# LayerNorm 1 of a transformer trunk: rows normalised by ScalarE, gamma and beta applied behind the transpose and again by GpSimd on the way down

## The chip, the cores and the metric

The kernel runs on one core of a Trainium2 chip. The metric is the time of the whole kernel on the device in microseconds (us), as the median of several executions; lower is better. The engines are PE (TensorE, matmuls and transposes), DVE (VectorE), ACT (ScalarE), POOL (GpSimd) and SP (SyncE, which here issues all the transfers). Each engine works through its own list of instructions strictly in order.

## The reference

One layer on x of 1024 rows by 1024 columns, all in float32. Two attentions share one input projection; their projected outputs are gated and added, and one output projection follows. Then come two residual LayerNorms with a SwiGLU feed-forward (FFN) of 2816 hidden columns between them:

```python
mix = (gate_a * y_a + gate_b * y_b) @ w_out[l]
x = layer_norm(DEEPNORM_ALPHA * x + mix, ln1_g[l], ln1_b[l])
gu = x @ w_ffn_in[l]
g, u = jnp.split(gu, 2, axis=-1)
ffn = (jax.nn.silu(g) * u) @ w_ffn_out[l]
x = layer_norm(DEEPNORM_ALPHA * x + ffn, ln2_g[l], ln2_b[l])
```

Here layer_norm subtracts a row's mean, divides by its standard deviation, multiplies by gamma and adds beta, both of which belong to columns. The LN1 output is used twice: as the FFN's input and, scaled by DEEPNORM_ALPHA, as the residual of LN2.

## The kernel before, in words

Rows are handled in eight tiles of 128 (0 to 7), columns in two halves of 512, LO and HI. All large products are made with a Strassen-like scheme of seven half-size products, run in the order 5, 1, 3, 6, 2, 7, 4. Each float32 operand is split into a high part (a cast by ACT, L112) and a low part (the difference, by DVE, L113), and each product is three matmuls. A list scheduler fixes the order of every engine's instructions when the kernel is built, from its own costs; names such as op, yt, kp or QKV are sets of SBUF buffers, and a tile waits until its buffer is free.

The stages: input projection and gates, attention, output projection (`ops`, L1134, to about 788 us), LN1 and its transposes, FFN up (L179, 22 blocks of hidden columns, to 1219 us), FFN down (`dn`, L1275), LN2.

**LN1.** When a row tile's last product is taken from PSUM (L1125, L1127), DVE makes the statistics (L968, L969), adds epsilon (L970), and POOL raises the variance to the power -0.5 (L971). DVE then does (t - mean) * gamma on the full row (L972). In tiles 1 to 3 and 5 to 7 DVE goes on with times 1/std plus beta in two halves (L975); in tiles 0 and 4 ACT scales (L979) and POOL adds beta (L980). The finished row is stored to DRAM for the residual (`x1_dr`). When four row tiles are done, PE transposes them in 128x128 blocks (L995, `x1ps`), two banks of 512 for each of four steps. From each bank ACT casts the high part and DVE subtracts for the low part (`x1A`, `split`, L112 and L113). ACT also copies the first half's banks to `x1raw` (L1002) and four of the second half's to `x1s` (L1012), 16 casts and 12 copies in all; DVE makes sums of these (L1013, L1014, L1020, L1021), which are split again into the other products' operands.

**FFN up to down.** DVE and ACT make the hidden activations h; POOL makes sums of them (`sa`, `sb`, L1072 to L1078), which go to DRAM (`left_dr`).

**FFN down.** 77 steps, eleven for each product, each of 12 matmuls (L1275). A step needs a left operand `dl` (from `raw`, reloaded h sums) and a right operand `dr` (from `rows`, the weights, or from sums of these: `t` on L1237, `rows` on L1239 and L1240). Each is cast by ACT and subtracted by DVE, into a ring of eight buffers (QKV), so operands of four steps are held at a time. SP loads the rows nine steps ahead. Steps 3 to 10 of the first product each also load one row tile of the LN1 output (L1313, tiles 4 to 7, then 0 to 3) as `x`. After each product DVE takes its four banks from PSUM: the first product into the HI half of tiles 4 to 7, the second into the LO half of tiles 0 to 3 (L1125, alpha * x + bank).

Of the kernel before, what the change touches and what calls it, by code (L numbers as in the profile page):

```python
# [48 lines left out]

@with_exitstack  # L50
def hybrid_trunk_kernel(ctx: ExitStack, tc, x, xt, w_in, w_v, b_gate, rel_bias, w_proj,
                        w_out, ln1_g, ln1_b, w_ffn_in, w_ffn_out, ln2_g, ln2_b, out):

# [57 lines left out]
    def split(dst_h, dst_l, src):  # L111
        nc.scalar.copy(dst_h, src)  # L112
        nc.vector.tensor_tensor(dst_l, src, dst_h.bitcast(F32), ALU.subtract)  # L113
# [185 lines left out]
    def small_inputs():  # L299

        rel_sb = cycle(QK, "rel_sb")[0:8, 0:896]
        rel_in = cycle(QK, "rel_in")[0:8, 0:N_REL]
# [4 lines left out]
        dma(bg, b_gate)

    def store_hl(d, hi, lo):
        for h in range(2):  # L310
# [650 lines left out]
        dma(t, bass.AP(tensor=src.tensor, offset=src.offset, ap=[[0, P], [1, D]]))  # L961
        return t

    def layer_norm(t, g, b, name, quick, done=lambda cs: None):
        st = sml.tile([P, 12], F32, name=f"bn_{name}", tag="bn")
        mv = sml.tile([P, 3], F32, name=f"mv_{name}", tag="mv")
        for hf in range(2):
            nc.vector.bn_stats(st[:, 6 * hf:6 * hf + 6], t[:, hf * HW:(hf + 1) * HW])  # L968
        nc.vector.bn_aggr(mv[:, 0:2], st)  # L969
        nc.vector.tensor_scalar(mv[:, 2:3], mv[:, 1:2], EPS, None, ALU.add)  # L970
        nc.gpsimd.tensor_tensor(mv[:, 2:3], mv[:, 2:3], neghalf, ALU.pow)  # L971
        nc.vector.scalar_tensor_tensor(t, t, mv[:, 0:1], g, ALU.subtract, ALU.mult)  # L972
        if quick:
            for cs in (LO, HI):
                nc.vector.scalar_tensor_tensor(t[:, cs], t[:, cs], mv[:, 2:3], b[:, cs],  # L975
                                               ALU.mult, ALU.add)
                done(cs)
        else:
            nc.scalar.activation(t, t, AF.Copy, scale=mv[:, 2:3])  # L979
# [8 lines left out]
    def x1_operands(hf, acc_t):

        for kt in range(4):  # L990
            tps = []
            for k in (kt, kt + 4):
                tp = bank("tr", f"x1ps{hf}_{k}")
                for j in range(4):
                    tr(tp[:, j * P:(j + 1) * P], acc_t[4 * hf + j][:, k * P:(k + 1) * P], ident)  # L995
                tps.append(tp)
            if hf == 0:
                raw = slot("bw", f"x1raw{kt}")
                for i in range(2):
# [4 lines left out]
                x1raw.append(raw)
            else:
                raw = x1raw[kt]
                for i in range(2):
# [1 line left out]
                    split(o[:, LO], o[:, HI], tps[i])
                    ops_hi[i].append((o[:, LO], o[:, HI]))  # L1010
                s13 = slot("kp", f"x1s13_{kt}")
                nc.scalar.copy(s13[:, LO], tps[1])  # L1012
                nc.vector.tensor_tensor(s13[:, HI], raw[:, LO], tps[0], ALU.subtract)  # L1013
                nc.vector.tensor_tensor(s13[:, LO], tps[0], s13[:, LO], ALU.add)  # L1014
                x1s13.append(s13)
# [366 lines left out]
```

## Time and profile before

| what | value |
|---|---|
| median of three runs | 1431.96 us |
| lowest and highest run | 1430.93 and 1436.22 us |
| the profiled execution | 1438.71 us |
| its span in the trace | 1436.9 us |
| PE, DVE, ACT, POOL busy | 1405.3, 1024.1, 689.4, 309.9 us |
| granted TensorE clock, mean | 0.996 of full speed |

A row of a timeline has the start in us, the duration, the engine, the line, the operation, the tiles written and read, their shapes, and in brackets the idle time before it with what ended that. Back-to-back instructions of an engine overlap a little, so the distance of two starts is shorter than a duration. Rows of one kind are put together with their count (x3), and a count can be a little low, since some matmul records are missing. A grouped row has the total busy time, the mean of one in ns, and the idle time before the group with what ended most of it. Idle time of an engine that nobody waits for costs nothing.

### The profile page before, as it was taken

The numbers are of one execution on the slowest core, as the hardware profiler recorded it, in microseconds if no ns is written. First come the engines' busy times: TensorE is split into PE (matmuls) and PEld (weight loads), VectorE is DVE, ScalarE is ACT, GpSimd is POOL, SyncE is SP. The second block draws the span as 40 slices with busy tenths as digits, with TensorE's granted clock in tenths as the row PEclk, the third lists the DMA queues.
The fourth block names the chain that finished last, engine by engine and source line by source line (L and its number), as shares of the span: only waits on it lengthen the run. The fifth ranks groups of instructions, "written<-read, shape, count | busy, mean of one in ns | idle before, by whom it ended". The sixth has DMA issues, their size and how long they took to land.

```text
span 1436.9 us, 18884 instructions
## 1 busy us (share of the span) xinstructions
PE 1405.3 (98%) x6592; PEld 1159.7 (81%) x6592; DVE 1024.1 (71%) x1596; ACT 689.4 (48%) x1203; POOL 309.9 (22%) x365
## 2 busy tenths in 40 slices
PE   8999999999999998999999999999999999999997
PEld 6888888888778787888888878888888888888886
DVE  8866467773887987897779995555555544785996
ACT  6444354554888876783233543333333332444540
POOL 0000000000565775771303031111111100300012
PEclk9999999999999999999999999999999999999999
DMA  7565737888787559888862143223322227853521
GB/s 249 169 179 181 234 91 275 300 320 302 201 234 226 168 161 278 269 269 301 312 236 85 69 139 125 94 104 110 110 87 91 95 100 251 316 192 110 174 81 73
DMA packets 102895, 264.49 MB, mean 184 GB/s; under 512 B 10880, under 2 KB 27264, under 8 KB 102800
## 3 DMA queue, kind: packets, MB, share of 16 engines
q1 hardware_dynamic: 102800, 263.29, 55.3%
q8 instruction: 52, 0.85, 0.2%
q14 instruction: 43, 0.35, 0.1%
HBM read 172.25 MB, written 90.99 MB: 183 GB/s over the span
## 4 chain that ended last, share of the span: by engine, by line
PE 83%; DVE 8%; DMA 3%; ACT 3%; issue 2%; POOL 1%; POOLq 0%; SPq 0%; DVEq 0%; ACTq 0%
PE dn L1275 15%; PE sxf L179 14%; PE sxp L179 8%; PE szf L179 6%; PE v L431 5%; PE ops L1134 5%; PE szp L179 4%; PE gps L572 4%; PE syf L179 4%; PE yAps L793 2%; PE syp L179 2%; PE tp_b L730 2%; PE tp_a L730 1%; DMA wRf<-in_w_ffn_in_dram 1%; DMA yh<-y_dr2h 1%
## 5 line engine op out<-in xcount | busy, mean ns | idle before, releaser
L1275 PE MATMUL dn<-dr,dl 128*128 128x512 f32 x924 | 209.6, 389 | 0.0
L1275 PEld LDWEIGHTS dn<-dr,dl 128*128 128x128 f32 x924 | 173.4, 188 | 36.0
L704 POOL TENSOR_TENSOR w_b<-w_b,kp_b 128x511 f32<-128x511 f32 (+3 forms) x96 | 103.8, 1085 | 53.0 <-DVE kp_b L701 49.5
L701 DVE TENSOR_TENSOR_SCAN kp_b<-kp_b,ident_ps 128x512 f32<-128x512 f32 (+3 forms) x96 | 92.7, 966 | 4.0 <-ACT kp_b L699 1.4
L112 ACT CAST dl<-raw 128x512 fp32r<-128x512 f32 x77 | 47.5, 623 | 84.7 <-PE dn L1275 68.6
L1134 PE MATMUL ops<-wr,wl 128*128 128x512 f32 x336 | 78.8, 392 | 0.0
L971 POOL TENSOR_TENSOR mv<-mv,neghalf 128x1 f32<-128x1 f32 x16 | 25.6, 1603 | 242.0 <-DVE mv L970 242.0
L1134 PEld LDWEIGHTS ops<-wr,wl 128*128 128x128 f32 x336 | 62.5, 188 | 12.5
L653 POOL MEMSET bias<- 64x64 f32 x8 | 1.2, 146 | 330.1 <-ACT bias L652 330.1
L113 DVE TENSOR_TENSOR dl<-raw,dl 128x512 fp32r<-128x512 f32 x77 | 53.3, 699 | 24.8 <-ACT dl L112 24.2
L674 POOL TENSOR_SCALAR w_a<-w_a,st_a 128x640 f32<-128x640 f32 (+2 forms) x64 | 46.6, 734 | 75.9 <-PE sc_a L634 38.5
L113 DVE TENSOR_TENSOR pt_b<-tp_b,pt_b 128x512 fp32r<-128x512 f32 (+1 forms) x80 | 49.9, 630 | 16.7 <-ACT pt_b L112 15.8
L112 ACT CAST pt_b<-tp_b 128x512 fp32r<-128x512 f32 (+1 forms) x80 | 44.2, 554 | 36.6 <-PE tp_b L730 36.2
L1072 POOL TENSOR_TENSOR sb<-h 128x512 f32<-128x512 f32 x10 | 20.2, 2021 | 185.6 <-PE syf L179 135.1
L179 PE MATMUL szf<-x1S63h,wcf 128*128 128x512 f32 x168 | 55.1, 389 | 0.0
L192 DVE TENSOR_TENSOR gt<-sxf,gt 128x512 f32<-128x512 f32 x21 | 14.4, 686 | 54.9 <-PE sxf L179 54.9
L671 ACT ACTIVATE w_a<-w_a,st_a 128x640 f32<-128x640 f32 (+2 forms) x64 | 44.7, 699 | 13.2 <-DVE st_a L666 11.8
L699 ACT ACTIVATE kp_b<-sc_b 128x512 f32<-128x512 f32 (+3 forms) x96 | 49.0, 511 | 1.5 <-PE sc_b L634 1.4
L700 ACT ACTIVATE w_b<-sc_b 128x511 f32<-128x511 f32 (+3 forms) x96 | 49.1, 512 | 0.0
L1073 POOL TENSOR_TENSOR sa<-h,h 128x512 f32<-128x512 f32 x10 | 15.9, 1586 | 143.0 <-PE sxf L179 120.3
L730 PEld LDWEIGHTS tp_b<-ident,w_b 128*128 128x128 f32 x288 | 36.6, 141 | 12.1 <-issue 1.0
L730 PE MATMUL tp_a<-ident,w_a 128*128 128x128 f32 x240 | 41.9, 277 | 4.4 <-POOL w_a L674 2.5
(1525 smaller groups left out, 4188.2 us busy)
## 6 DMA issues: line engine op xcount, KB each, us to landing
raw<-left_dr SPq DMA_DIRECT2D x77, 256.0 KB, 2.9
wo_dr<-wo SPq DMA_DIRECT2D x28, 512.0 KB, 3.9
wr<-wo_dr SPq DMA_DIRECT2D x28, 512.0 KB, 8.7
wLf<-in_w_ffn_in_dram SPq DMA_DIRECT2D x22, 512.0 KB, 4.4
wRf<-in_w_ffn_in_dram SPq DMA_DIRECT2D x22, 512.0 KB, 4.3
rows<-in_w_ffn_out_dram SPq DMA_DIRECT2D x22, 512.0 KB, 6.3
left_dr<-h SPq DMA_DIRECT2D x33, 256.0 KB, 2.0
v_dr<-vst SPq DMA_DIRECT2D x16, 512.0 KB, 3.2
```

What stands on the lines that cost most here:

```text
L112: nc.scalar.copy(dst_h, src)
L113: nc.vector.tensor_tensor(dst_l, src, dst_h.bitcast(F32), ALU.subtract)
L179: mm(acc, lw[:, ks], rx, start=(first and kt == i == 0), stop=(kt == 3 and i == 2), skip_group_check=not first)
L431: mm(banks[mt], xs[lw][:, ms], o[:, rx], start=(fresh and kt == n == 0), stop=(kt == 3 and n == 2), skip_group_check=not fresh)
L572: mm(acc, lw[:, ks], rx[k][:, cs], start=(k == j == 0), stop=(k == KT - 1 and j == 2))
L699: nc.scalar.activation(kp[:, c0:e], sc[:, 0:n], AF.Sigmoid, scale=-1.0)
L700: nc.scalar.activation(be[:, m0:e], sc[:, m0 - c0:n], AF.Sigmoid)
L701: nc.vector.tensor_tensor_scan(kp[:, c0:e], kp[:, c0:e], ident_ps()[:, 0:n], kp[:, c0 - 1:c0] if c0 else 0.0, ALU.mult, ALU.bypass if c0 e ...
L704: nc.gpsimd.tensor_tensor(be[:, m0:e], be[:, m0:e], kp[:, m0 - 1:e - 1], ALU.mult)
L730: tr(tp[:, j:j + P], wt[qb - q0][:, (kb - qb) * P:(kb - qb + 1) * P], ident)
L1134: mm(acc, lw, rx, start=(fresh and n == m == 0), stop=(n == 3 and m == 2), skip_group_check=not fresh)
L1275: mm(acc, lw, rx, start=(fresh and steps[s][1] == n == 0), stop=(last and n == 2), skip_group_check=not fresh)
```

## The change

All eight row tiles of LN1 go one way. After the power DVE makes -mean/std (a 128x1 operation), and one ACT instruction normalises the full row with that as bias and 1/std as scale, both per partition. No gamma or beta is applied to rows there. Behind the transpose columns lie on partitions, so ACT applies gamma and beta from PSUM as a scale and a bias per partition, once into the high part and once, in full, into `x1raw` or `x1s13`; DVE's low part is the difference of those two, both in SBUF. The two sums of `x1s13` now read SBUF only. The rows stored to DRAM are without gamma and beta; on the way down POOL applies them to each reloaded row, in four instructions of 128x512. Gamma and beta by column are loaded into two yt buffers at down step 1 and no longer before LN1; by partition they come once more, as a small constant of 128x16 (gb1).

```diff
-    def layer_norm(t, g, b, name, quick, done=lambda cs: None):
+    def row_stats(t, name):
...
+        mv = sml.tile([P, 4], F32, name=f"mv_{name}", tag="mv")
...
+    def normalise(t, name):
+        mv = row_stats(t, name)
+        nc.vector.scalar_tensor_tensor(mv[:, 3:4], mv[:, 0:1], -1.0, mv[:, 2:3],
+                                       ALU.mult, ALU.mult)
+        nc.scalar.activation(t, t, AF.Identity, bias=mv[:, 3:4], scale=mv[:, 2:3])
+
+    def layer_norm(t, g, b, name, done):
+        mv = row_stats(t, name)
         nc.vector.scalar_tensor_tensor(t, t, mv[:, 0:1], g, ALU.subtract, ALU.mult)
-        if quick:
-            for cs in (LO, HI):
-                nc.vector.scalar_tensor_tensor(t[:, cs], t[:, cs], mv[:, 2:3], b[:, cs],
-                                               ALU.mult, ALU.add)
-                done(cs)
-        else:
-            nc.scalar.activation(t, t, AF.Copy, scale=mv[:, 2:3])
-            nc.gpsimd.tensor_tensor(t, t, b, ALU.add)
-            done(slice(0, D))
+        for cs in (LO, HI):
+            nc.vector.scalar_tensor_tensor(t[:, cs], t[:, cs], mv[:, 2:3], b[:, cs],
+                                           ALU.mult, ALU.add)
+            done(cs)
...
+    def affine(dst, src, k):
+        nc.scalar.activation(dst, src, AF.Identity, bias=gb1[:, 8 + k:9 + k],
+                             scale=gb1[:, k:k + 1])
...
-                for i in range(2):
-                    o = slot("xt", f"x1A1{i}_{kt}", F32R)
-                    split(o[:, LO], o[:, HI], tps[i])
-                    nc.scalar.copy(raw[:, (LO, HI)[i]], tps[i])
-                    ops_1[1 + i].append((o[:, LO], o[:, HI]))
+                dst = (raw[:, LO], raw[:, HI])
...
+                affine(o[:, LO], tps[i], kt + 4 * i)
+                affine(dst[i], tps[i], kt + 4 * i)
+                nc.vector.tensor_tensor(o[:, HI], dst[i], o[:, LO].bitcast(F32), ALU.subtract)
...
-            layer_norm(acc_t[tt], g1, b1, f"1_{tt}", tt % 4 >= 1)
+            normalise(acc_t[tt], f"1_{tt}")
...
+        if s == 1:
+            norm1 = [bcast(src, slot("yt", f"ln1{n}")) for src, n in ((ln1_g, "g"), (ln1_b, "b"))]
         if p == 5 and i >= 3:
             tt = (i + 1) % 8
             acc_t[tt] = slot("op", f"x1_{tt}")
             dma(acc_t[tt], x1_dr[tt])
+            for cs in (HI, LO):
+                t = acc_t[tt][:, cs]
+                nc.gpsimd.tensor_tensor(t, t, norm1[0][:, cs], ALU.mult)
+                nc.gpsimd.tensor_tensor(t, t, norm1[1][:, cs], ALU.add)
```

Lines move by the insertions: L971 becomes L973, L995 L1007, L1134 L1146, L1127 L1139, L113 L114, L1237 L1249, L1239 L1251, L1313 L1327. New are L979 (DVE, -mean/std), L981 (ACT, the row), L997 (ACT, affine from PSUM), L1025 (DVE, low part), L1330 and L1331 (POOL, gamma and beta). The scheduler places all of it anew.

DVE's list at row tile 2 of LN1, before (here acc_7249 is tile 2 and acc_7250 tile 3):

```order
L1127 TENSOR_TENSOR acc_7249<-ops_2_7645,acc_7249 128x512
L968 BN_STATS bn_2_7659<-acc_7249 128x6
L968 BN_STATS bn_3_7684<-acc_7250 128x6
L969 BN_AGGR mv_2_7660<-bn_2_7659 128x2
L970 TENSOR_SCALAR mv_2_7660<-mv_2_7660 128x1
L972 SCALAR_TENSOR_TENSOR acc_7249<-acc_7249,mv_2_7660,ln1g 128x1024
L1127 TENSOR_TENSOR acc_7250<-ops_3_7670,acc_7250 128x512
L975 SCALAR_TENSOR_TENSOR acc_7249<-acc_7249,mv_2_7660,ln1b 128x512 x2
```

The same place in the changed kernel (acc_7251 is tile 2, acc_7252 tile 3):

```order
L1139 TENSOR_TENSOR acc_7251<-ops_2_7641,acc_7251 128x512
L970 BN_STATS bn_2_7655<-acc_7251 128x6
L970 BN_STATS bn_3_7679<-acc_7252 128x6
L971 BN_AGGR mv_2_7656<-bn_2_7655 128x2
L972 TENSOR_SCALAR mv_2_7656<-mv_2_7656 128x1
L979 SCALAR_TENSOR_TENSOR mv_2_7656<-mv_2_7656 128x1
L1139 TENSOR_TENSOR acc_7252<-ops_3_7665,acc_7252 128x512
L970 BN_STATS bn_3_7679<-acc_7252 128x6
```

The full-row operation that stood behind L970, and needs only the mean, is gone, and L979, which reads POOL's power, stands there with the next tile's take behind it.

PE's list where row tile 2 is first transposed, before (acc_7247 to acc_7249 are tiles 0 to 2):

```order
L995 MATMUL x1ps_1_7714<-ident,acc_7247 128x128
L995 MATMUL x1ps_1_7714<-ident,acc_7248 128x128
L1134 MATMUL ops_0_7351<-wr_0_7459,wl_0_7499 128x512 x3
L1134 MATMUL ops_0_7351<-wr_1_7461,wl_1_7502 128x512 x3
L1134 MATMUL ops_0_7351<-wr_2_7463,wl_2_7505 128x512
L995 MATMUL x1ps_0_7695<-ident,acc_7249 128x128
L995 MATMUL x1ps_1_7714<-ident,acc_7249 128x128
```

And in the changed kernel (acc_7249 to acc_7251 are tiles 0 to 2):

```order
L1007 MATMUL x1ps_1_7708<-ident,acc_7249 128x128
L1007 MATMUL x1ps_1_7708<-ident,acc_7250 128x128
L1146 MATMUL ops_0_7349<-wr_0_7457,wl_0_7497 128x512 x3
L1007 MATMUL x1ps_0_7689<-ident,acc_7251 128x128
L1007 MATMUL x1ps_4_7694<-ident,acc_7251 128x128
L1007 MATMUL x1ps_1_7708<-ident,acc_7251 128x128
L1146 MATMUL ops_0_7349<-wr_1_7459,wl_1_7500 128x512 x3
```

Tile 2 is now wanted after three matmuls of the output projection instead of seven.

POOL's list from the last sums of the FFN up to LN2, before:

```order
L1075 TENSOR_TENSOR sa_10879<-h_10723,h_10822 128x512
L1076 TENSOR_TENSOR sb_10880<-h_10723 128x512
L1077 TENSOR_TENSOR sa_10879<-sa_10879,h_10723 128x512
L1078 TENSOR_TENSOR sb_10880<-h_10822,sa_10879 128x512
L971 TENSOR_TENSOR mv_0_12344<-mv_0_12344,neghalf 128x1
```

And in the changed kernel, with the first three of the row tiles:

```order
L1087 TENSOR_TENSOR sa_10873<-h_10717,h_10816 128x512
L1088 TENSOR_TENSOR sb_10874<-h_10717 128x512
L1089 TENSOR_TENSOR sa_10873<-sa_10873,h_10717 128x512
L1090 TENSOR_TENSOR sb_10874<-h_10816,sa_10873 128x512
L1330 TENSOR_TENSOR x_4_11024<-x_4_11024,ln1g 128x512 x2
L1331 TENSOR_TENSOR x_4_11024<-x_4_11024,ln1b 128x512 x2
L1330 TENSOR_TENSOR x_5_11052<-x_5_11052,ln1g 128x512 x2
L1331 TENSOR_TENSOR x_5_11052<-x_5_11052,ln1b 128x512 x2
L1330 TENSOR_TENSOR x_6_11079<-x_6_11079,ln1g 128x512 x2
L1331 TENSOR_TENSOR x_6_11079<-x_6_11079,ln1b 128x512 x2
```

Thirty-two instructions of 128x512, four for each of the eight row tiles, stand between the FFN sums and the first power of LN2, where nothing stood.

More of the change, by code (lines that the diff above doesn't have):

```diff
@@ L51, in hybrid_trunk_kernel @@
 def hybrid_trunk_kernel(ctx: ExitStack, tc, x, xt, w_in, w_v, b_gate, rel_bias, w_proj,
-                        w_out, ln1_g, ln1_b, w_ffn_in, w_ffn_out, ln2_g, ln2_b, out):
+                        w_out, ln1_g, ln1_b, ln1_c, w_ffn_in, w_ffn_out, ln2_g, ln2_b, out):
     nc = tc.nc
@@ L94, in hybrid_trunk_kernel @@
     bg = cst.tile([P, 16], F32, name="bg")
+    gb1 = cst.tile([P, 16], F32, name="gb1")
     q_dr = [dr.tile([2 * P, S], F32, name=f"q_dr{i}") for i in range(8)]
@@ L307, in small_inputs @@
         dma(bg, b_gate)
+        dma(gb1, ln1_c)
     def store_hl(d, hi, lo):
@@ L962, in bcast @@
         return t
-    def layer_norm(t, g, b, name, quick, done=lambda cs: None):
+    def row_stats(t, name):
         st = sml.tile([P, 12], F32, name=f"bn_{name}", tag="bn")
-        mv = sml.tile([P, 3], F32, name=f"mv_{name}", tag="mv")
+        mv = sml.tile([P, 4], F32, name=f"mv_{name}", tag="mv")
         for hf in range(2):
@@ L971, in layer_norm @@
         nc.gpsimd.tensor_tensor(mv[:, 2:3], mv[:, 2:3], neghalf, ALU.pow)
-        nc.vector.scalar_tensor_tensor(t, t, mv[:, 0:1], g, ALU.subtract, ALU.mult)
-        if quick:
-            for cs in (LO, HI):
-                nc.vector.scalar_tensor_tensor(t[:, cs], t[:, cs], mv[:, 2:3], b[:, cs],
-                                               ALU.mult, ALU.add)
-                done(cs)
-        else:
-            nc.scalar.activation(t, t, AF.Copy, scale=mv[:, 2:3])
-            nc.gpsimd.tensor_tensor(t, t, b, ALU.add)
-            done(slice(0, D))
+        return mv
+    def normalise(t, name):
[5 more added lines that the diff above has]
+        mv = row_stats(t, name)
+        nc.vector.scalar_tensor_tensor(t, t, mv[:, 0:1], g, ALU.subtract, ALU.mult)
+        for cs in (LO, HI):
+            nc.vector.scalar_tensor_tensor(t[:, cs], t[:, cs], mv[:, 2:3], b[:, cs],
+                                           ALU.mult, ALU.add)
+            done(cs)
     ops_1 = {p: [] for p in range(1, 8)}
@@ L1006, in x1_operands @@
                 raw = x1raw[kt]
-                for i in range(2):
-                    o = slot("bw", f"x1A22_{kt}", F32R) if i else cycle(QKV, f"x1A12_{kt}", F32R)
[L1009 to L1015, printed above, removed]
+                s13 = slot("kp", f"x1s13_{kt}")
+                dst = (s13[:, HI], s13[:, LO])
+                x1s13.append(s13)
+            for i in range(2):
+                if hf == 0:
+                    o = slot("xt", f"x1A1{i}_{kt}", F32R)
+                else:
+                    o = slot("bw", f"x1A22_{kt}", F32R) if i else cycle(QKV, f"x1A12_{kt}", F32R)
+                affine(o[:, LO], tps[i], kt + 4 * i)
+                affine(dst[i], tps[i], kt + 4 * i)
+                nc.vector.tensor_tensor(o[:, HI], dst[i], o[:, LO].bitcast(F32), ALU.subtract)
+                (ops_1[1 + i] if hf == 0 else ops_hi[i]).append((o[:, LO], o[:, HI]))
+            if hf:
+                nc.vector.tensor_tensor(s13[:, LO], s13[:, HI], s13[:, LO], ALU.add)
+                nc.vector.tensor_tensor(s13[:, HI], raw[:, LO], s13[:, HI], ALU.subtract)
     def x1_sums(kt):
@@ L1030, in hybrid_trunk_kernel @@
         dma(acc_t[tt], x[tt * P:(tt + 1) * P, :])
-    g1 = bcast(ln1_g, slot("kp", "ln1g"))
-    b1 = bcast(ln1_b, slot("kp", "ln1b"))
     Wf = [dict() for _ in range(NF)]
@@ L1281, in end_row @@
     def end_row(tt):
-        layer_norm(acc_t[tt], *norm2, f"2_{tt}", True,
+        layer_norm(acc_t[tt], *norm2, f"2_{tt}",
                    lambda cs: dma(out[tt * P:(tt + 1) * P, cs], acc_t[tt][:, cs]))
@@ L1364, in layout @@
         w_out=arr["w_out"], ln1_g=arr["ln1_g"], ln1_b=arr["ln1_b"],
+        ln1_c=np.concatenate([arr[n].reshape(8, P).T for n in ("ln1_g", "ln1_b")], 1),
         w_ffn_in=granules(arr["w_ffn_in"]), w_ffn_out=arr["w_ffn_out"],
```

## The prediction

> **What bounds the kernel now.** I read the page first (busy times, then the chain that ended last), then windows on the two places where the change puts instructions, then PE's waits there, and last the timelines of VectorE (DVE) and GpSimd (POOL). The page:
>
> ```profile
> PE 1405.3 (98%) x6592; PEld 1159.7 (81%) x6592; DVE 1024.1 (71%) x1596; ACT 689.4 (48%) x1203; POOL 309.9 (22%) x365
> PE 83%; DVE 8%; DMA 3%; ACT 3%; issue 2%; POOL 1%; POOLq 0%; SPq 0%; DVEq 0%; ACTq 0%
> L1275 PE MATMUL dn<-dr,dl 128*128 128x512 f32 x924 | 209.6, 389 | 0.0
> ```
>
> PE is busy for 1405.3 of 1436.9 us, so taking work from another engine pays only where PE waits for it, and all waits of PE together are 31.6 us. The windows are the stretches of the LN1 rows, the transposes, the first and the later steps down; the columns are the length, then busy time and count of PE, PEld, DVE, ACT and POOL, the granted clock, the DMA share and GB/s.
>
> ```profile
> 745.00:800.00 55.00, 54.74 (x263) 44.02 (x262) 48.75 (x82) 14.52 (x24) 17.20 (x10) 1.00 0.29 116
> 800.00:860.00 60.00, 58.18 (x264) 47.00 (x262) 58.84 (x74) 33.98 (x45) 11.44 (x4) 1.00 0.33 106
> 1235.00:1282.00 47.00, 47.00 (x209) 38.93 (x208) 38.54 (x64) 19.43 (x34) 0.00 (x0) 1.00 0.86 310
> 1282.00:1310.00 28.00, 28.00 (x125) 23.19 (x124) 14.62 (x24) 12.11 (x22) 0.00 (x0) 1.00 0.32 104
> ```
>
> PE never stops in the last two, and loses 0.26 and 1.82 us in the first two. Its waits from 700 to 860 (total, times, longest):
>
> ```profile
> PE sxf L179 <- DVE gt L192: 1.8, 2, 1.4
> PE x1ps L995 <- DVE acc L975: 0.3, 1, 0.3
> ```
>
> So 2.1 us is all that a faster LN1 can win, though DVE is nearly full there. The down stage has nothing to win: PE is full, DVE has 8.46 us free in 47, POOL does nothing.
>
> **The rows of LN1.** The change takes from DVE eight full-row operations and twelve half-rows (busy, mean ns, idle ahead):
>
> ```profile
> L972 DVE SCALAR_TENSOR_TENSOR acc<-acc,mv,ln1g 128x1024 f32<-128x1024 f32 x8 | 10.2, 1275 | 0.0
> L975 DVE SCALAR_TENSOR_TENSOR acc<-acc,mv,ln1b 128x512 f32<-128x512 f32 x12 | 8.4, 743 | 0.4 <-POOL mv L971 0.4
> ```
>
> That frees 18.6 us of DVE, less eight tiny 128x1 operations at about 0.2 (L970 below has 0.15). But the order puts each of these directly behind the variance step, and it reads what POOL's power gives. Row 2, DVE then POOL:
>
> ```profile
> 760.11 0.69 DVE L1127 TENSOR_TENSOR acc<-ops,acc 128x512 f32<-128x512 f32 x1
> 760.84 1.29 DVE L968 BATCH_NORM_STATS2 bn<-acc 128x6 f32<-128x512 f32 x2
> 762.04 0.19 DVE L969 BATCH_NORM_AGGREGATE mv<-bn 128x2 f32<-128x12 f32 x1
> 762.27 0.15 DVE L970 TENSOR_SCALAR mv<-mv 128x1 f32<-128x1 f32 x1
> 762.34 1.28 DVE L972 SCALAR_TENSOR_TENSOR acc<-acc,mv,ln1g 128x1024 f32<-128x1024 f32 x1
> ```
> ```profile
> 762.50 1.52 POOL L971 TENSOR_TENSOR mv<-mv,neghalf 128x1 f32<-128x1 f32 x1 [3.92 <-DVE mv L970]
> ```
>
> Before, L972 covered the power. Now DVE stands still from 762.4 to 764.0, with the next row's take and statistics queued behind it; over eight rows that is about 13 us of the 18.6 freed. ScalarE (ACT) then normalises the row. The nearest row is L979, with one pointer operand instead of two:
>
> ```profile
> L979 ACT ACTIVATE acc<-acc,mv 128x1024 f32<-128x1024 f32 x2 | 2.3, 1153 | 10.4 <-POOL mv L971 10.4
> L112 ACT CAST x1A<-x1ps 128x512 fp32r<-128x512 f32 x16 | 9.2, 595 | 33.0 <-PE x1ps L995 33.0
> ```
>
> Row 2 is thus ready at 764.02 + 0.2 (DVE) + 1.25 (ACT) + 0.1, or 765.6. PE in that place:
>
> ```profile
> 762.64 0.82 PE L995 MATMUL x1ps<-ident,acc 128*128 128x128 f32 x6
> 763.22 1.84 PE L1134 MATMUL ops<-wr,wl 128*128 128x512 f32 x7
> 764.93 0.44 PE L995 MATMUL x1ps<-ident,acc 128*128 128x128 f32 x2
> ```
>
> Before, seven matmuls lay between the transposes of rows 0 and 1 and the first of row 2, and PE reached them at 764.93. In the new order three do: 763.2 plus 3 x 0.24 is 763.9, a stall of 1.7. PE itself set the 760.11 (twelve matmuls of the next row, 2.7 us, lie between the end of row 2's and 762.64), so the freed DVE doesn't bring row 2 earlier. Row 3's statistics begin when DVE comes free at 764.2: 0.6 for its take, 0.6 for half the statistics, 0.4, the power 1.6, and 1.5 as above make 768.9; PE is there after row 2's three transposes and eight matmuls, 765.6 + 0.3 + 1.95 = 767.9, so 1.0 more. The second half of the rows (6 and 7) has the same pattern in the order: twice 2.7 is 5.4. Behind the transposes two affine passes take the place of a cast and a copy, 32 ACT operations from PSUM for 28; at 0.595, the cast's row, ACT keeps its pace. If each took 0.75, a bank of 512 costs 1.5 on ACT against four transposes and some four matmuls on PE, 4 x 0.1 + 4 x 0.24 or 1.36: up to 2.3 us over sixteen banks. I take zero, by the cast's row, and keep 2.3 for the range. The Trainium skill's "ScalarE: Activation LUTs", section "What ACT_TABLE_LOAD costs", has 93 ns for each per-partition pointer operand; by it an affine is an estimated 0.78 us, and the LN1 term would be about 2 us dearer. No row here has two such operands.
>
> Sum for LN1: +5.4, less the 2.1 of waits that may go: +3.3, between -2.1 (order covers the power) and +8.
>
> **The way down.** POOL gets 32 operations of 128x512 with two SBUF inputs (eight rows by four). They start when the rows of x land, and the takes of the first four rows need them:
>
> ```profile
> x<-x_dr SPq DMA_DIRECT2D x8, 512.0 KB, 5.4
> 1219.35 21.02 PE L1275 MATMUL dn<-dr,dl 128*128 128x512 f32 x92
> 1250.15 1.87 DVE L1125 SCALAR_TENSOR_TENSOR x<-x,dn 128x512 f32<-128x512 f32 x3
> ```
>
> POOL works on them from about 1234 on (its own sums, below, end there), in the window where DVE is 82% busy, 56 of its 64 operations sums of two SBUF inputs (all but the eight of L1125, below). What that does is in the trace, where POOL's last sums of the FFN run beside the first steps down; DVE, then POOL:
>
> ```profile
> 1225.78 0.68 DVE L113 TENSOR_TENSOR dl<-raw,dl 128x512 fp32r<-128x512 f32 x1
> 1226.38 0.68 DVE L113 TENSOR_TENSOR dr<-t,dr 128x512 fp32r<-128x512 f32 x1
> 1227.09 1.67 DVE L1237 TENSOR_TENSOR t<-rows 128x512 f32<-128x512 f32 x1
> 1228.68 1.77 DVE L113 TENSOR_TENSOR dl<-raw,dl 128x512 fp32r<-128x512 f32 x1
> 1230.38 1.78 DVE L113 TENSOR_TENSOR dr<-t,dr 128x512 fp32r<-128x512 f32 x1
> 1232.20 1.66 DVE L1237 TENSOR_TENSOR t<-rows 128x512 f32<-128x512 f32 x1
> ```
> ```profile
> 1221.49 6.72 POOL L1075 TENSOR_TENSOR sa<-h,h 128x512 f32<-128x512 f32 x1 [32.83 <-DVE h L1116]
> 1228.17 1.74 POOL L1076 TENSOR_TENSOR sb<-h 128x512 f32<-128x512 f32 x1
> 1229.87 1.74 POOL L1077 TENSOR_TENSOR sa<-sa,h 128x512 f32<-128x512 f32 x1
> ```
>
> Alone, DVE starts one every 0.60 us (1225.78, 1226.38); beside POOL every 1.70 (1228.68, 1230.38). They take turns, one POOL operation delaying DVE by 1.10. Where DVE reads PSUM they don't hinder each other:
>
> ```profile
> 880.12 0.69 DVE L192 TENSOR_TENSOR gt<-syf,gt 128x512 f32<-128x512 f32 x1 [2.22 <-PE syf L179]
> 879.12 1.30 POOL L1077 TENSOR_TENSOR sa<-sa,h 128x512 f32<-128x512 f32 x1
> 880.50 1.29 POOL L1078 TENSOR_TENSOR sb<-h,sa 128x512 f32<-128x512 f32 x1
> ```
>
> The Trainium skill's "SBUF — State Buffer", section "Who interferes with whom", has GpSimd and a VectorE instruction with two SBUF inputs exclude each other for a whole instruction, and one SBUF input leave VectorE out of it. The rows agree with both, and the sum by it is the one below. L1075's 6.72 us, behind a dense run of DVE work, is longer than one instruction; that is a rival below.
>
> So 32 x 1.10 = 35.2 us of DVE delay. What falls into DVE's free time costs nothing:
>
> ```profile
> L1239 DVE TENSOR_TENSOR rows<-rows,rows 128x512 f32<-128x512 f32 x8 | 5.5, 684 | 7.0 <-DMA rows<-in_w_ffn_out_dram 7.0
> L1125 DVE SCALAR_TENSOR_TENSOR x<-x,dn 128x512 f32<-128x512 f32 x8 | 5.1, 679 | 0.0
> L112 ACT CAST dl<-raw 128x512 fp32r<-128x512 f32 x17 | 10.6, 624 | 26.8 <-PE dn L1275 26.8
> ```
>
> That is 7.0 of waits for rows, and about 2 of the 5.1 in takes from PSUM: 26 us are left. The third row gives DVE's lead over PE: casts wait for PE to end the step four back, since eight buffers hold four steps. A step is 209.6 / 77 = 2.72 us, so operands stand ready at most 3 x 2.72, less 1.9 for two casts and two subtractions, 6.3 us ahead; POOL's sums before 1234 have used some, I take 5. PE loses 26 - 5 = 21 us. From below: 32 x 1.15 of POOL and 56 x 0.60 of DVE are 70.4 us on one path with 47 + 6.3 to spend, 17. If a turn costs DVE 0.85 and not 1.10, 27 - 9 - 5 = 13; if nothing falls into the gaps, 35 - 5 = 30. It is not won back: behind 1282 PE was full.
>
> The rest I cost at nothing. The loads of gamma and beta move to SP's queue ahead of the last step-down rows; they wait for a buffer that the DVE work ahead of L1075 frees at about 1221, and one load of weight rows queued behind them is used after 1240 (step 10 of 2.72 us from 1219.35 begins at 1246.6); one more small load lies in the early stage. If DMA, at 0.86, gives the added 1 MB only after the rows, it is 3 us more, inside the range.
>
> **Sum.** +3.3 and +21, about +25: the profiled execution, 1438.71 us with a span of 1436.9, would become 1464, and the median of the runs, 1431.96, becomes 1457.
>
> **Rivals.**
> 1. POOL shut out (0.15). As L1075 did, POOL gets in only where DVE pauses, and the first takes, due at 1250.15, find unfinished rows; DVE waits there for POOL, which takes 1.38 apiece undisturbed (879.12 to 880.50). Sixteen take 22 us, most of them from 1250 on, and the takes of the other four rows, eleven steps later, wait once more; after gaps and lead about +24 to +30: 1459 to 1466. Against it: L1076 and L1077 alternate.
> 2. Hidden, not slower (0.16). POOL's work falls into the 8.46 us of free DVE time, the turns and the lead, so PE never runs dry. This decides if a collision costs DVE under (9 + 6.3) / 32 = 0.48 us. Then only LN1 is left: +3.3, 1435, or, if the freed DVE ends both waits and no row stalls, -2.1: 1430. Against it: four collisions at 1.10 in the rows above.
> 3. ACT becomes the limit at the transposes (0.05): LN1 at +8, together with 21 or more, 1461 to 1468. For it, two affine passes per bank; against it, ACT's 14.52 busy of 55.
>
> A gain beyond 0.5% would need 7.2 us (0.5% is about what a measurement of this kernel can tell from no change), where only 2.1 of waits lie: 0.04, for what I don't see. The forecast has 0.60. Slower is 0.60 + 0.15 + 0.05. Range: 13 - 2.1 below, reached on to 1438 for part of the hidden case, and 30 + 6 above: 1438 to 1468.
>
> **What would show it.** In the changed profile: POOL busy 1235 to 1290, its L1330 and L1331 at about 1.7 us and not 1.29; DVE's L114 and L1251 near 1.7 in pairs with it; PE waiting about 20 us for dl or dr there; DVE's L979 waiting 1.6 us per row for POOL, and PE's L1007 waiting at four places in 760 to 802. I am wrong if PE stays full from 1235 to 1310.

## The result, and the profile after

| | before | changed |
|---|---|---|
| median of 5 runs | 1431.66 us | 1453.9 us |
| lowest and highest | 1430.93 to 1436.22 | 1450.15 to 1455.0 |
| span of the profiled execution | 1436.9 us | 1452.9 us |

The ratio is 1.0145, with a 95% interval of 1.0124 to 1.0167: slower by 1.5%, or 22.2 us between the medians. 1457 had been forecast.

PE's group for the way down now has a wait of 12.6 us in it, which had been 0.0 (total busy time, mean ns of one, idle time ahead). Its busy time grew too, from 209.6 us by 7.9, in part at a lower granted clock. The windows are those shown of before:

```profile
L1287 PE MATMUL dn<-dr,dl 128*128 128x512 f32 x924 | 217.5, 397 | 12.6 <-DVE dr L114 12.6
```
```profile
745.00:800.00 55.00, 53.65 (x263) 42.65 (x263) 37.45 (x75) 35.12 (x44) 4.11 (x8) 1.00 0.19 77
800.00:860.00 60.00, 57.72 (x254) 47.12 (x253) 53.58 (x65) 29.08 (x38) 7.92 (x5) 1.00 0.38 118
1235.00:1282.00 47.00, 34.35 (x130) 25.57 (x128) 46.93 (x32) 12.72 (x23) 47.00 (x29) 0.91 0.58 199
1282.00:1310.00 28.00, 28.00 (x113) 23.04 (x114) 24.54 (x39) 10.23 (x18) 1.02 (x1) 0.91 0.57 189
```

Read the third row against its counterpart. PE had 47.00 of 47 and has 34.35; DVE had 38.54 in 64 operations and has 46.93 in 32. Half as many operations fill more time. POOL is busy for all 47 us. The granted clock fell from 1.00 to 0.91. In the first two rows PE is hardly touched, though DVE's load there fell from 48.75 to 37.45 and from 58.84 to 53.58 (the same work lies some 7 us earlier in this execution, so these two pairs are only roughly alike).

The two profiled executions also differ by something that isn't the change: that of before has a wait of 4.7 us for a load in the attention stage (PE yAps <- DMA yh), where this one has 0.3. So I compare from the first matmul of the output projection to the end, by the first and last start of these groups, before and then after:

```profile
L1134 PE MATMUL ops<-wr,wl x336: 387/389/481, 708.2 to 788.2; 128*128 128x512 f32 x168
L1275 PE MATMUL dn<-dr,dl x924: 388/389/389, 1219.4 to 1428.6; 128*128 128x512 f32 x185
```
```profile
L1146 PE MATMUL ops<-wr,wl x336: 387/389/478, 701.3 to 782.3; 128*128 128x512 f32 x168
L1287 PE MATMUL dn<-dr,dl x924: 387/389/796, 1214.8 to 1444.5; 128*128 128x512 f32 x185
```

From `ops` to the way down 511.2 us became 513.5, so +2.3; the way down itself, 209.2, became 229.7, so +20.5, which is the 12.6 and the 7.9 of PE's group. Together that is 22.8, near the 22.2 of the medians.

The way down in the changed kernel, POOL, then DVE, then PE (in brackets the idle time before and what ended it):

```profile
1229.43 3.32 POOL L1330 TENSOR_TENSOR x<-x,ln1g 128x512 f32<-128x512 f32 x2 [0.69 <-DMA x<-x_dr]
1232.70 3.44 POOL L1331 TENSOR_TENSOR x<-x,ln1b 128x512 f32<-128x512 f32 x2
...
1279.65 3.38 POOL L1331 TENSOR_TENSOR x<-x,ln1b 128x512 f32<-128x512 f32 x2
```
```profile
1233.21 1.78 DVE L114 TENSOR_TENSOR dr<-t,dr 128x512 fp32r<-128x512 f32 x1
1234.92 1.78 DVE L114 TENSOR_TENSOR dl<-raw,dl 128x512 fp32r<-128x512 f32 x1
1236.62 1.78 DVE L114 TENSOR_TENSOR dr<-t,dr 128x512 fp32r<-128x512 f32 x1
```
```profile
1260.07 3.02 PE L1287 MATMUL dn<-dr,dl 128*128 128x512 f32 x12 [0.33 <-DVE dr L114]
1266.81 4.51 PE L1287 MATMUL dn<-dr,dl 128*128 128x512 f32 x12 [3.72 <-DVE dr L114]
1273.55 4.55 PE L1287 MATMUL dn<-dr,dl 128*128 128x512 f32 x12 [2.23 <-DVE dr L114]
1281.95 58.43 PE L1287 MATMUL dn<-dr,dl 128*128 128x512 f32 x246 [3.86 <-DVE dr L114]
```

POOL and DVE take turns from 1229.4 to 1283.0. Of POOL's 32 operations 29 start 1.67 to 1.71 us after the one before; one comes after 1.58, and one, while DVE takes banks from PSUM, after 1.26. PE has its lead until 1245, then runs at DVE's pace, one step of 12 matmuls for every two to five turns. After the last wait it never stops again.

In LN1, around row tile 2 (DVE, POOL, ACT, PE):

```profile
755.35 0.15 DVE L972 TENSOR_SCALAR mv<-mv 128x1 f32<-128x1 f32 x1
756.17 0.16 DVE L979 SCALAR_TENSOR_TENSOR mv<-mv 128x1 f32<-128x1 f32 x1 [0.66 <-POOL mv L973]
```
```profile
755.59 0.55 POOL L973 TENSOR_TENSOR mv<-mv,neghalf 128x1 f32<-128x1 f32 x1 [4.89 <-DVE mv L972]
```
```profile
756.36 1.24 ACT L981 ACTIVATE acc<-acc,mv 128x1024 f32<-128x1024 f32 x1 [4.20 <-DVE mv L979]
```
```profile
757.66 0.55 PE L1007 MATMUL x1ps<-ident,acc 128*128 128x128 f32 x3 [0.42 <-ACT acc L981]
```

The chain is the one forecast, and PE waits at its end, but for 0.42 us and not 1.7: the power takes 0.55, not 1.52. PE's waits from 700 to 870 are now these:

```profile
PE sxf L180 <- DVE gt L193: 1.6, 1, 1.6
PE x1ps L1007 <- ACT acc L981: 1.3, 4, 0.5
PE sxf L180 <- ACT h L206: 0.7, 1, 0.7
```

### The profile page after: what moved, and what is told of

The parts are those of the page before. It is cut to its first block, busy times and chain, and to the rows that moved or that the text cites. A ratio compares the mean times of both kernels' runs of the same rounds, so it can differ in the third digit from the quotient of the medians.

```text
span 1452.9 us, 18932 instructions
## 1 busy us (share of the span) xinstructions
PE 1411.1 (97%) x6592; PEld 1160.4 (80%) x6592; DVE 1041.9 (72%) x1584; ACT 704.0 (48%) x1213; POOL 347.0 (24%) x395
## 4 chain that ended last, share of the span: by engine, by line
PE 79%; DVE 10%; DMA 5%; issue 2%; ACT 2%; POOL 1%; SPq 0%; POOLq 0%; DVEq 0%; ACTq 0%
PE sxf L180 14%; PE dn L1287 13%; PE sxp L180 8%; PE szf L180 6%; PE v L433 5%; PE ops L1146 5%; PE szp L180 4%; PE syf L180 4%; PE gps L574 3%; PE yAps L795 2%; PE syp L180 2%; PE tp_b L732 2%; DMA wRf<-in_w_ffn_in_dram 1%; PE tp_a L732 1%; PE yBps L120 1%
## 5 line engine op out<-in xcount | busy, mean ns | idle before, releaser
L1287 PE MATMUL dn<-dr,dl 128*128 128x512 f32 x924 | 217.5, 397 | 12.6 <-DVE dr L114 12.6
L1287 PEld LDWEIGHTS dn<-dr,dl 128*128 128x128 f32 x924 | 176.9, 192 | 53.0 <-DVE dr L114 16.0
L113 ACT CAST dl<-raw 128x512 fp32r<-128x512 f32 x77 | 47.6, 622 | 105.1 <-PE dn L1287 89.6
L114 DVE TENSOR_TENSOR dl<-raw,dl 128x512 fp32r<-128x512 f32 x77 | 64.2, 840 | 20.6 <-ACT dl L113 20.3
L1146 PE MATMUL ops<-wr,wl 128*128 128x512 f32 x336 | 78.5, 392 | 0.0
L1146 PEld LDWEIGHTS ops<-wr,wl 128*128 128x128 f32 x336 | 62.5, 188 | 12.6
L973 POOL TENSOR_TENSOR mv<-mv,neghalf 128x1 f32<-128x1 f32 x16 | 18.1, 1132 | 223.2 <-DVE mv L972 223.2
L114 DVE TENSOR_TENSOR pt_b<-tp_b,pt_b 128x512 fp32r<-128x512 f32 (+1 forms) x80 | 49.8, 630 | 13.7 <-ACT pt_b L113 12.8
L1084 POOL TENSOR_TENSOR sb<-h 128x512 f32<-128x512 f32 x10 | 14.6, 1457 | 188.1 <-PE syf L180 150.9
L113 ACT CAST pt_b<-tp_b 128x512 fp32r<-128x512 f32 (+1 forms) x80 | 43.7, 549 | 32.3 <-PE tp_b L732 31.3
L114 DVE TENSOR_TENSOR dr<-rows,dr 128x512 fp32r<-128x512 f32 x66 | 53.1, 813 | 0.8 <-ACT dr L113 0.7
L155 DVE TENSOR_TENSOR taf<-wRf,wLf 128x512 f32<-128x512 f32 x21 | 14.5, 691 | 45.5 <-DMA wRf<-in_w_ffn_in_dram 45.5
```

The lines of the kernel that those rows point to most:

```text
L1146: mm(acc, lw, rx, start=(fresh and n == m == 0), stop=(n == 3 and m == 2), skip_group_check=not fresh)
L1287: mm(acc, lw, rx, start=(fresh and steps[s][1] == n == 0), stop=(last and n == 2), skip_group_check=not fresh)
```

## The experiments

Theory: the time is lost on the way down, because each GpSimd operation there delays a VectorE operation with two SBUF inputs by 1.10 us. Rivals: LN1's own stalls, or the moved loads.

**1. The change without GpSimd's operations on the way down.** The residual then lacks gamma and beta.

```diff
-            for cs in (HI, LO):
-                t = acc_t[tt][:, cs]
-                nc.gpsimd.tensor_tensor(t, t, norm1[0][:, cs], ALU.mult)
-                nc.gpsimd.tensor_tensor(t, t, norm1[1][:, cs], ALU.add)
```

> The changed kernel without GpSimd's 32 operations on the way down; the loads of gamma and beta stay, the residual of LayerNorm 2 lacks gamma and beta. Theory (each of the 32 delays VectorE by 1.10 us, which empties PE and then lowers its clock): the stretch down takes 209 us again instead of 230, PE full from 1235 to 1310 at clock 1.00, time 1453.9 - 20.6 = 1433 (1431 to 1436). Rival 1 (LayerNorm 1 itself and its stalls cost the time): 1448 or more. Rival 2 (the loads of gamma and beta ahead of the weight rows starve the first steps): 1443 to 1454, and VectorE waits for DMA rows.

Measured: 1432.72 us beside 1431.38 for the kernel before, ratio 1.0013 (1.0004 to 1.0023). PE on the way down:

```profile
1213.03 137.30 PE L1287 MATMUL dn<-dr,dl 128*128 128x512 f32 x605
```
```profile
1235.00:1282.00 47.00, 47.00 (x209) 38.92 (x208) 37.71 (x62) 20.18 (x36) 0.00 (x0) 1.00 0.82 287
```

One unbroken run, and DVE is back at 62 operations in 37.71 us. Both rivals fall: the loads are still there, and everything in the change but these operations is worth +0.13%, about 1.9 us.

**2. The kernel before, with GpSimd's operations added on the way down.** The residual then gets gamma and beta twice.

```diff
+        if s == 1:
+            norm1 = [bcast(src, slot("yt", f"ln1{n}")) for src, n in ((ln1_g, "g"), (ln1_b, "b"))]
...
+            for cs in (HI, LO):
+                t = acc_t[tt][:, cs]
+                nc.gpsimd.tensor_tensor(t, t, norm1[0][:, cs], ALU.mult)
+                nc.gpsimd.tensor_tensor(t, t, norm1[1][:, cs], ALU.add)
```

> The kernel before, its LayerNorm 1 untouched, with the changed kernel's two loads and 32 GpSimd operations put on the way down (so gamma and beta are applied twice to the residual). Theory: the stretch down loses as much as in the changed kernel, 1431.7 + 20.6 = 1452 (1449 to 1456). Rival 1 (LayerNorm 1 costs the time): 1432 to 1436.

Measured: 1451.44, ratio 1.0141 (1.0125 to 1.0158), or +20.2 us. PE's wait on the way down has the same size as in the changed kernel:

```profile
PE dn L1275 <- DVE dr L113: 12.7, 8, 3.9
```

The two parts add up: 1.9 and 20.2 are 22.1, beside 20.8 by the ratio of the whole change and 22.2 by the medians.

**3. The same operations on VectorE.**

```diff
-                nc.gpsimd.tensor_tensor(t, t, norm1[0][:, cs], ALU.mult)
-                nc.gpsimd.tensor_tensor(t, t, norm1[1][:, cs], ALU.add)
+                nc.vector.tensor_tensor(t, t, norm1[0][:, cs], ALU.mult)
+                nc.vector.tensor_tensor(t, t, norm1[1][:, cs], ALU.add)
```

> The changed kernel with the same 32 operations on VectorE instead of GpSimd. Theory (a GpSimd operation delays VectorE by 1.10 us, its own takes 0.60): 32 x 0.60 = 19.2 of VectorE, less 9 in its free time and 5 of lead, PE loses about 5, 1438 (1434 to 1443): giving the work to the idle engine is dearer than doing it. Rival (any 32 more operations on that path cost the same, whoever does them): 1452 to 1456.

Measured: 1437.9, ratio 1.005 (1.0032 to 1.0069). DVE does them at its usual pace, and PE waits five times for 0.6 to 0.8 us:

```profile
L1331 DVE TENSOR_TENSOR x<-x,ln1b 128x512 f32<-128x512 f32 x12 | 7.7, 689 | 0.0
```
```profile
PE dn L1287 <- DVE dr L114: 3.2, 5, 0.8
```

So work that DVE does itself in 0.60 us costs it 1.10 when POOL does it alongside. The same 32 operations take 5.2 us of the kernel's time on DVE and some 20 on POOL.

**4. GpSimd with one SBUF input.** The residual lacks gamma and beta again.

```diff
-                nc.gpsimd.tensor_tensor(t, t, norm1[0][:, cs], ALU.mult)
-                nc.gpsimd.tensor_tensor(t, t, norm1[1][:, cs], ALU.add)
+                nc.gpsimd.tensor_scalar(t, t, 1.0, None, ALU.mult)
+                nc.gpsimd.tensor_scalar(t, t, 0.0, None, ALU.add)
```

> The changed kernel with GpSimd's 32 two-input operations replaced by 32 with one SBUF input (times 1.0, plus 0.0), so the residual lacks gamma and beta. The trace has 0.73 us for such an operation of 640 columns, so 0.6 for 512. Theory (GpSimd shuts VectorE's second input out for as long as it reads): each turn costs VectorE about 0.5, 32 x 0.5 - 14 = 2 of PE, 1436 (1433 to 1441). Rival A (only two-input operations collide): VectorE's L114 stays at 0.68 and the time is 1433. Rival B (a turn costs the same whatever GpSimd does): 1450 or more.

Measured: 1440.53, ratio 1.0068 (1.0042 to 1.0094). Inside the bounds named, 4.5 above the value. DVE beside such operations, then POOL's group, then DVE's takes:

```profile
1230.17 1.10 DVE L114 TENSOR_TENSOR dr<-t,dr 128x512 fp32r<-128x512 f32 x1
1231.19 0.68 DVE L114 TENSOR_TENSOR dl<-raw,dl 128x512 fp32r<-128x512 f32 x1
1231.79 1.09 DVE L114 TENSOR_TENSOR dr<-t,dr 128x512 fp32r<-128x512 f32 x1
```
```profile
L1330 POOL TENSOR_SCALAR x<-x 128x512 f32<-128x512 f32 x16 | 26.4, 1667 | 1.0 <-DMA x<-x_dr 1.0
```
```profile
L1137 DVE SCALAR_TENSOR_TENSOR x<-x,dn 128x512 f32<-128x512 f32 x4 | 2.6, 680 | 6.0 <-POOL x L1331 6.0
```

Every second DVE operation is 0.42 us longer, so a collision costs DVE 0.42 and not 1.10; rivals A and B both fall. But POOL's operation takes 1.67, not the 0.6 assumed, and so the rows are late: DVE waits 6.0 us for POOL at the takes. The 0.6 came from a group of 0.73 that mixes widths: at 640 columns alone it has 0.80 in this run. Most of the 1.67 isn't the collision: such an operation at 1252.37, while DVE stood still, took 1.49. Why that is so much more than 0.80 isn't settled.

**5. Why the power was shorter.** A full-row DVE operation that changes nothing, put where L972 had been:

```diff
+        nc.vector.scalar_tensor_tensor(t, t, mv[:, 0:1], t, ALU.min, ALU.max)
         nc.vector.scalar_tensor_tensor(mv[:, 3:4], mv[:, 0:1], -1.0, mv[:, 2:3],
```

> The changed kernel with a full-row VectorE operation of two SBUF inputs that leaves the row as it is (min with the mean, then max with itself) between the variance step and the small product, where the kernel before had its (t - mean) * gamma. It asks why GpSimd's power took 1.5 us before and 0.55 in the changed kernel. Theory (that operation shut GpSimd out of the second port): the power takes 1.5 again in all eight rows, and PE's waits for rows at the transposes grow from 1.3 us to 3 to 6. Rival (the power is shorter for another reason, such as its place or its values): it stays at 0.55.

Measured: 1457.39, ratio 1.0183 (1.0169 to 1.0197). POOL's power and DVE's operation, row tile 2:

```profile
760.59 1.52 POOL L973 TENSOR_TENSOR mv<-mv,neghalf 128x1 f32<-128x1 f32 x1 [3.92 <-DVE mv L972]
```
```profile
760.42 1.27 DVE L979 SCALAR_TENSOR_TENSOR acc<-acc,mv 128x1024 f32<-128x1024 f32 x1
762.14 0.16 DVE L980 SCALAR_TENSOR_TENSOR mv<-mv 128x1 f32<-128x1 f32 x1 [0.44 <-POOL mv L973]
```

All eight powers take 1.46 to 1.54 again, so the 1.52 of the kernel before was itself a collision. The second part of the expectation was missed: PE's waits for rows grew to 1.9 us, not 3 to 6, because the scheduler again placed seven matmuls ahead of row tile 2's transposes.

**6. Gamma and beta in FFN up.** If the way down has no room, perhaps FFN up has. A row tile per block is reloaded into the kp buffers, treated and stored again, by GpSimd with ACT's normalisation (6a), by VectorE with a VectorE normalisation (6b), and by GpSimd with that (6c).

```diff
...
+            if j == 2 and 5 <= f < 13:
+                xr = slot("kp", f"xr{f}")
+                dma(xr, x1_dr[f - 5])
+                xrs.append(xr)
+            if j == 4 and 5 <= f < 13:
+                for cs in (HI, LO):
+                    t = xrs[-1][:, cs]
+                    nc.gpsimd.tensor_tensor(t, t, norm1[0][:, cs], ALU.mult)
+                    nc.gpsimd.tensor_tensor(t, t, norm1[1][:, cs], ALU.add)
+            if j == 2 and 6 <= f < 14:
+                dma(x1a_dr[f - 6], xrs[f - 6])
...
```

Not shown are the loads of gamma and beta into two kp buffers, now in FFN up, and the way down, which loads the treated rows from `x1a_dr` and has no such operations left. In 6b `nc.vector` stands for `nc.gpsimd`. In 6b and 6c the normalisation is:

```diff
-        nc.vector.scalar_tensor_tensor(mv[:, 3:4], mv[:, 0:1], -1.0, mv[:, 2:3],
-                                       ALU.mult, ALU.mult)
-        nc.scalar.activation(t, t, AF.Identity, bias=mv[:, 3:4], scale=mv[:, 2:3])
+        nc.vector.tensor_scalar(t, t, mv[:, 0:1], mv[:, 2:3], ALU.subtract, ALU.mult)
```

> The changed kernel with GpSimd's 32 operations moved into FFN up (blocks 5 to 12, one row tile each, reloaded, given gamma and beta in free buffers, stored again). The collisions stay, 32 x 1.10 = 35 us of VectorE, but spread over eight blocks of about 19 us in which VectorE is little more than half busy: 4.4 us each. Theory (only where VectorE has no room does a collision reach PE): 1433 + 0 to 4, and GpSimd's operations are longer than 1.3 only beside two-input ones. Rival (collisions cost PE wherever they lie): 1445 or more.

> As the kernel before this one of the list, but VectorE applies gamma and beta in FFN up, 32 x 0.60 = 19.2 us over eight blocks, and VectorE normalises the rows with one two-scalar operation (subtract, multiply) instead of the small product and ScalarE's pass. Theory: PE's four waits for ScalarE at the transposes (1.4 us) go, nothing comes back on the way down: 1431 (1429 to 1434). Rival (VectorE lacks the time in LayerNorm 1 or in FFN up): 1435 or more, with PE waiting for gt or the transposes' rows.

> As the one before, with GpSimd instead of VectorE for gamma and beta in FFN up. Theory: 1431 to 1435, no better than VectorE itself, since each of the 32 still delays VectorE by 1.10 against 0.60 for doing it. Rival (the idle engine is free where VectorE has room): 1 to 2 us below the VectorE version.

Measured: 1461.56 (ratio 1.0208, 1.0191 to 1.0224), 1440.05 (1.0063, 1.005 to 1.0075) and 1460.29 (1.0211, 1.0195 to 1.0227). All three expectations were missed, the GpSimd ones by some 25 us. The way down is undisturbed in each; PE waits in FFN up, here in 6a, with DVE's wait for a buffer in the same blocks, and DVE and ACT in the first of them:

```profile
PE sxf L181 <- ACT h L207: 18.7, 8, 4.1
```
```profile
DVE tbf L157 <- DMA x1a_dr<-xr: 10.5, 7, 2.2
```
```profile
889.78 1.77 DVE L1129 TENSOR_TENSOR h<-h,gt 128x512 f32<-128x512 f32 x1
891.48 1.77 DVE L156 TENSOR_TENSOR taf<-wRf,wLf 128x512 f32<-128x512 f32 x1
893.17 1.77 DVE L160 TENSOR_TENSOR taf<-wRf 128x512 f32<-128x512 f32 x1
897.16 0.69 DVE L157 TENSOR_TENSOR tbf<-wRf,taf 128x512 f32<-128x512 f32 x1 [2.21 <-DMA x1a_dr<-xr]
897.77 0.68 DVE L194 TENSOR_TENSOR gt<-syf,gt 128x512 f32<-128x512 f32 x1
```
```profile
898.48 0.63 ACT L1123 ACTIVATE gt<-gt 128x512 f32<-128x512 f32 x1 [7.83 <-DVE gt L194]
899.02 0.57 ACT L207 COPY h<-sxf 128x512 f32<-128x512 f32 x1
```

The DVE operation that ACT waits for, and PE behind it (L194), stands in DVE's list behind four others. The collisions make three of those 1.1 us later each, and L157 then waits for a buffer that a stored row still holds. Half-busy DVE is no room if the urgent work stands last in a burst. The long waits also cost clock: from 960 to 1050 us the granted clock was 0.94 in 6a and 1.00 in experiment 1. In 6b the transposes' rows now come late from DVE (2.2 us of PE's waits against 1.4 with ACT), and PE waits 6.4 us for sxf's readers, against 1.7 in experiment 1.

**7. Collisions and traffic apart.** 7a: only POOL work in FFN up, on a small tile of zeros; 7b: only the reloads and stores. Gamma and beta are left out of the residual in both: the second cut shows the lines that go, in 7a and in 7b on the way down, and 7b doesn't put them into FFN up.

```diff
+            if j == 4 and 5 <= f < 13:
+                with tc.issue_after(last_pool[0]):
+                    for _ in range(8):
+                        nc.gpsimd.tensor_tensor(scr, scr, scr, ALU.add)
```
```diff
-                    nc.gpsimd.tensor_tensor(t, t, norm1[0][:, cs], ALU.mult)
-                    nc.gpsimd.tensor_tensor(t, t, norm1[1][:, cs], ALU.add)
```

> The changed kernel without GpSimd's operations on the way down (the residual lacks gamma and beta), and with 64 GpSimd additions of 128x256 on a small tile of zeros in FFN up, behind the h sums of blocks 5 to 12: the port time of 32 operations of 512, but no reload, no store and no shared buffers. It asks why the version with gamma and beta in FFN up took 27 us more. Theory A (collisions alone, in bursts beside the operations that PE waits for): 1450 or more. Theory B (there VectorE waited seven times, 10.5 us, for the buffer that the store of a row still held, and PE behind it): 1433 to 1438. Between them, both.

> The counterpart: the rows are reloaded in FFN up into the shared buffers and stored again, but GpSimd's 32 operations are left out (the residual lacks gamma and beta). Theory A of the run before: 1433 to 1435. Theory B, or the transfers themselves: 1440 or more, with VectorE waiting for the store.

Measured: 1439.26 (1.0054, 1.004 to 1.0068) and 1434.06 (1.0019, 1.0007 to 1.003). 7a lies between the ranges of the two theories, 7b inside the 1433 to 1435 of theory A. Against 1432.72 of experiment 1 they cost 6.5 and 1.3 us, where 6a had cost 28.8. That doesn't show that collisions and traffic cost more together than apart, because 7a delays DVE far less than 6a. DVE's busy time tells it, with the same 1584 operations in all four runs:

| run | DVE busy | above experiment 1 | time above experiment 1 |
|---|---|---|---|
| experiment 1 | 1010.7 us | | |
| 6a | 1042.2 us | 31.5 us | 28.8 us |
| 7a | 1018.3 us | 7.6 us | 6.5 us |
| 7b | 1009.3 us | -1.4 us | 1.3 us |

In 6a and 7a alike nearly every us by which DVE's operations grew came back in the kernel's time; most of POOL's work in 7a delayed no DVE operation. Nor does the held buffer explain 6a by itself: in 6b DVE waits 10.1 us for it, beside 10.5 in 6a, and 6b cost 7.3 us. How the 28.8 divide between the collisions, the buffer and the clock is not settled, since no run has 6a's collisions without its buffers.

**8. Each half row when it is due.** Half rows are loaded apart: 16 operations by the end of the second product, eight in the third, eight in the fifth; by VectorE (8a) and by GpSimd (8b). `affine_row`, not shown, is the multiplication and addition on the half row.

```diff
+    def load_row(tt, cs):
+        with tc.issue_after(last_load[0]):
+            dma(acc_t[tt][:, cs], x1_dr[tt][:, cs])
+        affine_row(tt, cs)
...
-            dma(acc_t[tt], x1_dr[tt])
...
+            load_row(tt, HI if tt > 3 else LO)
...
+        if p == 3 and 2 <= i < 6:
+            load_row(i - 2, HI)
+        if p == 2 and 2 <= i < 6:
+            load_row(i + 2, LO)
```

> The changed kernel with gamma and beta on VectorE on the way down, and each half row loaded and treated only when its product is near: 16 of the 32 operations by the end of the second product, eight in the third, eight in the fifth. Theory (what counts is VectorE's room ahead of the takes: 8.5 us free and 5 of lead): 16 x 0.60 = 9.6 fits, so PE loses nothing, 1433 (1431 to 1436), against 1437.9 with all 32 early. Rival (the order or the extra half-row transfers cost as much): 1437 or more.

> The same with GpSimd. Theory: 16 x 1.10 = 17.6 less 9 and 5 leaves 4 of PE by the second product's end, the other 16 fall where VectorE is half idle: 1437 (1434 to 1442), against 1453.9 with all 32 early. Rival (each collision reaches PE): 1450 or more.

Measured: 1438.08 (1.0046, 1.0032 to 1.0059) and 1450.67 (1.0132, 1.0115 to 1.015). Both missed, on the rivals' side. DVE's in-order list in 8a has operations that wait for late half rows ahead of the splits, and PE pays for one of them:

```profile
DVE x L1318 <- DMA x<-x_dr: 6.3, 4, 2.4
```
```profile
1246.57 151.42 PE L1287 MATMUL dn<-dr,dl 128*128 128x512 f32 x659 [1.81 <-DVE dr L114]
1399.16 30.25 PE L1287 MATMUL dn<-dr,dl 128*128 128x512 f32 x132 [1.17 <-DVE x L1139]
```

In 8b the first sixteen cost PE four waits of 5.6 us together, near the 4 expected. The last eight delay DVE, whose list then has rows of LN2 ahead of the take that PE waits for at the end (read from the list; no run takes it apart):

```profile
PE dn L1287 <- DVE x L1139: 4.3, 1, 4.3
```

No version tried beats the kernel before; the nearest, experiment 1, leaves out work.

## Why the prediction was right, point by point

- **PE bounds the kernel, LN1 can win 2.1 us at most.** Right. DVE was relieved and PE got nothing for it.
- **LN1: +3.3 us.** The trace has +2.3 up to the way down, experiment 1 +1.9. The mechanism was right, four stalls at the transposes behind POOL's power, but its sizes were off on both sides, and that the sum came near is luck. The stalls, +5.4, measured 1.3. At row tile 2 it was 0.42 and not 1.7, and 0.97 of the difference is the power: its 1.52 was priced from a row in which L972, with two SBUF inputs, lay beside it (experiment 5), and the change takes that row away. The -2.1 of waits that were to go did not come: 1.6 and 0.7 us are still lost at sxf.
- **Affine operations at the cast's 0.595.** Too low: they took 0.81.

```profile
L997 ACT ACTIVATE x1A<-x1ps,gb 128x512 fp32r<-128x512 f32 x16 | 13.0, 813 | 0.8 <-PE x1ps L1007 0.8
```

  They start every 0.66 us, 1.32 for a bank, which keeps just within PE's 1.36, and PE shows no wait for them. The 0.78 estimated from the Trainium skill's "ScalarE: Activation LUTs", section "What ACT_TABLE_LOAD costs", was the better price. By the prediction's own working (twice 0.78 against 1.36, sixteen times) it would have meant 3.2 us and not about 2; neither came.
- **The way down: 35.2 us of DVE delay, PE loses 21.** Right in its mechanism: the stage grew by 20.5 us, and the same operations made the old kernel 20.2 us slower. Two parts of the sum were off and nearly cancel. DVE's busy time is 1041.9 us, against 1010.7 in experiment 1 with the same 1584 operations, so the delay was 31.2 and not 35.2; beside the takes from PSUM a POOL operation costs DVE less than a whole turn. PE's last wait ends at 1281.95, and from there to the last start, 1444.5, are 162.5 us, of which 2.5 are due to the clock (below). The same steps take 160.0 at full speed, so PE was 229.7 - 2.5 - 209.2 = 18.0 late by then: gaps, takes and lead gave back 13 of the 31, near the 14 of the sum. The other 2.5 had no term.
- **The signs named.** POOL's and DVE's 1.7 us, and four waits at the transposes, came. PE's wait for dl or dr was 12.6 us and not about 20; the rest of the 20.5 is in its matmuls, 7.9 us longer. DVE's L979 waited for POOL by about 0.7 us per row and not 1.6.
- **What cost nothing.** Right: with the loads alone (experiment 1) the way down has no wait.
- **Rival 1, POOL shut out.** It did not come: each of the 32 had its turn. Only the first of the FFN sums was kept out again, as before.
- **Rival 2, hidden.** It fell by its own condition, since a collision costs 1.10 and not under 0.48; with one input it costs 0.42 (experiment 4), and even there the time was 1440, since the rows came late.
- **Rival 3, ACT the limit.** ACT was busy for 35.12 of 55 us and kept pace.

## What to carry to other kernels

Price an operation on an idle engine by what it does to its neighbour: here a GpSimd operation with two SBUF inputs delays VectorE by 1.10 us, more than the 0.60 VectorE needs to do the work itself. When a duration comes from a row, look what ran beside it there, since a change may take that neighbour away. An engine's mean busy share doesn't tell whether there is room; look at what stands in its list ahead of the operation that the bounding engine waits for.
